# A bank of its own for the third product of a group's first pair, and a norm whose stream waits for GpSimd by a price

## The chip, the cores and the metric

The kernel runs on one core of one Trainium2 chip. The time is device microseconds of one launch. A core has a matrix engine (TensorE, PE in the profile; PEld is its loading of weights), VectorE (DVE), ScalarE (ACT), GpSimd (POOL), SyncE (SP, which here only starts transfers) and 16 DMA engines. Each engine works through its own list of instructions in the order in which the program was written; engines wait for each other by semaphores.

## What is computed

One layer of a streaming encoder for 512 prompt rows and 8 x 16 sample rows, 640 rows together, with 1024 channels in 32-bit floats:

```python
z = x @ w_in                                  # x is layer-normed; columns: xa, ya, glu, q, gates
out_a = (rg_lru(causal_conv(xa, width 4)) * gelu(ya)) @ proj_a
u = glu[:512] * sigmoid(glu[512:])            # D_CONV = 512 channels
v = causal_conv(u, width 31)
out_b = silu(layer_norm(v)) @ proj_b          # norm over the 512 channels
out_c = cross_attention(q, memory) @ proj_c   # 4 heads, 256 tokens; the samples have caches of their own
g = sigmoid(gates + b_gate)
x = layer_norm(alpha * x + (g0 * out_a + g1 * out_b + g2 * out_c) @ w_out)
x = layer_norm(alpha * x + (silu(x @ w_ffn_gate) * (x @ w_ffn_up)) @ w_ffn_down)
```

## The kernel before

Activations lie with channels on the 128 partitions and the 640 rows along the free axis, in two halves of 320 (`HT`). Each 32-bit operand is split into a high part, rounded to a shorter format, and a low part, the rest; a product is three matmuls (high x high, high x low, low x high). The split inputs are `xh` and `xl`; the split weights `wh` and `wl`, made of a loaded block `wr`: ScalarE copies the high part (`prep_hi`) and VectorE, in some steps GpSimd (L305), subtracts to get the low part (`prep_lo`).

The work of TensorE is a list of `Step` objects. A main loop goes through it: it prepares the weights of the steps to come, issues this step's matmuls, and issues its evacuation (`evac`) a while later. An ordinary step multiplies one block of weights by both halves and takes two PSUM banks, `pu`, of four. There is a second kind of tile, `pv`, with two banks each, of which there are two; `side` counts those in use, `room` waits for one and `over` gives one back.

The small work (convolutions, norms, softmax, recurrence) is written as streams, which are Python generators. After each piece of matmuls the loop calls `advance`. It holds a price for every instruction that is written and so a time for TensorE (`P`), VectorE (`V`) and ScalarE (`A`); it takes a stream on as long as the larger of the times of V and A lies behind P's. At a `yield None` a stream stops until the next call. The prices only decide the order in which instructions are written; on the chip semaphores decide when they run. GpSimd (`G`) has no price before the change.

Two places matter.

First, `ln_b_stream`, the norm over the convolution's channels, around 253 us of the span. `total` adds up four tiles of 128 x 640 on GpSimd (L853 and L855). The stream stops once, and then writes a product of the sum with `ones` on TensorE, which spreads the mean over the partitions. VectorE subtracts that from the tiles, ScalarE squares them, GpSimd adds up the squares, and after two stops a second product follows (five matmuls of 128 x 100), then a power on GpSimd and `token_row`, a set of transposes.

Second, `seven`. The gates and the FFN's products are done in pairs of two blocks of columns by a scheme with seven products instead of eight (Strassen's, in Winograd's form): m1 to m7, each of 12 matmuls of 128 x 320, eight with the high part of a weight and four with its low part. Some products are accumulated in one bank. `after` says what happens to each product: m1 is copied by ScalarE into `tmp["a"]`; m6 is added to that copy by VectorE, m7 to the result, and `put` writes the four quarters of the output, with a function (sigmoid for the gates, SiLU for the FFN's gate) by ScalarE at the end. A group's first pair (`first`; the gates' at 491 us, the FFN's at 686 us) has an order of its own: m1, m4, m2, m6, m5, m7, m3. There m2 goes on in the bank of m1 ("x", `opens` False): its first matmul may only run when ScalarE has copied m1, and ScalarE takes the function of the sum from that bank.

```python
    PRODUCTS = (("m1", "x", True, "11", "11"), ("m6", "y", True, "s2", "t2"), ("m2", "x", False, "12", "21"),
...
            products = [PRODUCTS[i] for i in (0, 5, 2, 1, 4, 3)] + [("m3", "x", True, "s4", "22")]
```

Of the kernel before, what the change touches and what calls it, by code (L numbers as in the profile page):

```python
# [11 lines left out]
OP = mybir.AluOpType  # L12
# [8 lines left out]
HT = T // 2  # L21
# [46 lines left out]
def elements(x):  # L68
    n = 1
    for d in x.shape[1:]:  # L70
        n *= d
    return n
# [10 lines left out]
    return (130 if name == "scalar_tensor_tensor" else 70) + n / 0.96  # L83


TABLES = {AF.Exp: "e", AF.Tanh: "esgl", AF.Sigmoid: "s", AF.Sqrt: "q", AF.Silu: "l", AF.Gelu_apprx_tanh: "g"}


# [21 lines left out]
class Slots:  # L110
# [7 lines left out]
    def get(self, shape, dtype=F32):  # L118
        if not self.free_list:
            raise RuntimeError("no slot is free")  # L120
        i = self.free_list.pop(0)
        self.low = min(self.low, len(self.free_list))
        self.count += 1
        x = self.pool.tile([128, T], dtype, name=f"s{i}_{self.count}", tag=f"s{i}", bufs=1)
        x = view(x, shape)
        self.at[id(x)] = (i, x)
        return x
# [16 lines left out]
def trunk(ctx, tc, x_prompt, x_sample, mem_prompt, state_conv_a, state_lru, state_conv_b, cache_mem_k, cache_mem_v,  # L144
# [4 lines left out]
          new_conv_a_s, new_lru_s, new_conv_b_s):  # L149
    nc = tc.nc  # L150
    V, A, P = Engine(nc.vector, price_vector), Engine(nc.scalar, price_scalar), Engine(nc.tensor, price_tensor)
    G, S = nc.gpsimd, nc.sync

    w_in, proj_a, proj_b, proj_c, w_out = w_in[0], proj_a[0], proj_b[0], proj_c[0], w_out[0]
    w_mem_k, w_mem_v = w_mem_k[0], w_mem_v[0]
# [21 lines left out]
    side = [0]  # L177

    def pv():
        assert side[0] < 2  # L180
        side[0] += 1
        return ps.tile([128, 2, 512], F32, name="pv", tag="v", bufs=2)

    def room(n=1):
        while side[0] + n > 2:
            yield None

    def over(n=1):
        side[0] -= n
# [126 lines left out]
    def flush():  # L316
        while pending:
            pending.pop(0)()
# [5 lines left out]

    def advance(few=False):

        for e in (V, A):
            e.time = max(e.time, state["since"])
        state["since"] = P.time
        for item in list(streams):  # L330
            name, gen = item
            if few and name not in often:
                continue
            while max(V.time, 0 if name in vector_next else A.time) < P.time:
                try:
                    c = next(gen)
                except StopIteration:
                    streams.remove(item)
                    done.add(name)
                    break  # L340
                vector_next.discard(name)
                if c is None:
                    break
                if c == "v":
                    vector_next.add(name)

    def until(cond):

        flush()
        for item in list(streams):  # L350
            while not cond():
                try:
                    next(item[1])
                except StopIteration:
                    streams.remove(item)
                    done.add(item[0])
                    break
        assert cond()
# [391 lines left out]
    first = {"glu": len(steps)}  # L750
# [99 lines left out]
    def ln_b_stream():  # L850
        def total(x):
            y = get([128, T])
            G.tensor_tensor(y, x[0], x[1], op=OP.add)  # L853
            for k in range(2, KC):
                G.tensor_tensor(y, y, x[k], op=OP.add)  # L855
            return y

        y = total(vb)
        yield 1
        yield None  # L860
        yield from room()
        p = pv()
        P.matmul(p[:, 0], ones, y[:, :512], start=True, stop=True)
        P.matmul(p[:, 1, :128], ones, y[:, 512:], start=True, stop=True)
        free(y)
        yield None
        over()
        sq = []
        for k in range(KC):
            V.tensor_sub(vb[k][:, :512], vb[k][:, :512], p[:, 0])  # L870
            V.tensor_sub(vb[k][:, 512:], vb[k][:, 512:], p[:, 1, :128])
            x = get([128, T])
            A.activation(x, vb[k], AF.Square)
            sq.append(x)
            yield 1
        y = total(sq)
        free(*sq)
        yield 1
        yield None
        yield None  # L880
        yield from room()
        p = pv()

        for t in range(5):
            P.matmul(p[:, 0, t * 100:(t + 1) * 100], y[:, t * 128:(t + 1) * 128], ones[:, :100], start=True, stop=True)
        free(y)
        yield None
        over()
        ve = small.tile([128, 5], F32, name="ve5")
        V.tensor_scalar(ve, p[:, 0, :500].rearrange("p (t n) -> p t n", n=100)[:, :, 0], EPS, None, op0=OP.add)  # L890
        rs = small.tile([128, 5], F32, name="rs5")
        G.tensor_tensor(rs, ve, mhalf[:, :5], op=OP.pow)
        yield 1
        yield from room()
        p = token_row(rs)
        yield None
        over()
        for k in range(KC):
            V.tensor_mul(vb[k][:, :512], vb[k][:, :512], p[:, 0])
            V.tensor_mul(vb[k][:, 512:], vb[k][:, 512:], p[:, 1, :128])  # L900
            yield 1
        for k in range(KC):
            A.activation(vb[k], vb[k], AF.Silu, scale=pb[:, k, 32:33], bias=pb[:, k, 33:34])
        yield 1
        for k in range(KC):
            hi, lo = get([128, T], F32R), get([128, T], F32R)
            split(hi, lo, vb[k])
            free(vb[k])
            bT[k] = (hi, lo)
            yield 1  # L910
# [596 lines left out]
    def seven(pair, put, following, first=False):  # L1507

        acc, tmp, late = {}, {}, []

        def fourth(p):
            put(0, 1, p, tmp["b"][:, 0], OP.subtract)

        def fifth(p):
            put(1, 1, p, tmp["b"][:, 0], OP.add)
            if first:
                V.tensor_tensor(tmp["a"][:, 1], tmp["a"][:, 1], p, op=OP.add)

        def after(n, p):
            if n == "m1":  # L1520
                tmp["a"], tmp["b"] = get([128, 2, HT]), get([128, 2, HT])
                copy(tmp["a"][:, 0], p)
            elif n == "m6":
                V.tensor_tensor(tmp["a"][:, 1], tmp["a"][:, 0], p, op=OP.add)
            elif n == "m2":
                put(0, 0, p, None, None)
            elif n == "m7":
                V.tensor_tensor(tmp["b"][:, 0], tmp["a"][:, 0], p, op=OP.add)
                for f in late:
                    f()  # L1530
            elif n in ("m4", "m5"):
                f = lambda: (fourth if n == "m4" else fifth)(p)
                if first:
                    late.append(f)
                else:
                    f()
            else:
                free(tmp["b"])
                put(1, 0, p, tmp["a"][:, 1], OP.add)
                free(tmp["a"])  # L1540

        products = PRODUCTS
        if first:

            products = [PRODUCTS[i] for i in (0, 5, 2, 1, 4, 3)] + [("m3", "x", True, "s4", "22")]
        for i, (n, u, opens, xn, wn) in enumerate(products):
            def mm(w, u=u, opens=opens, xn=xn):
                if opens:
                    acc[u] = pu(1)[0][:, :HT]
                p = acc[u]  # L1550
                hi, lo = w
                xhi, xlo = quarters[xn]
                for k in range(half):
                    P.matmul(p, hi[:, k], xhi[k], start=opens and k == 0, stop=False, skip_group_check=not opens)
                    P.matmul(p, hi[:, k], xlo[k], start=False, stop=False, skip_group_check=not opens)
                yield
                for k in range(half):
                    P.matmul(p, lo[:, k], xhi[k], start=False, stop=k == half - 1, skip_group_check=not opens)
                yield

            before = None
            if first and i == 0:
                before = sums_there
            elif first and i == 2 and following:
                before = lambda: (following.sums_1(), following.sums_2())
            elif following and not first and i == 2:
                before = following.sums_1
            elif following and not first and i == 3:
                before = following.sums_2
            Step(pair.ld, (lambda r, wn=wn: pair.block(wn)), [128, half, 128], mm,  # L1570
                 (lambda n=n, u=u: after(n, acc[u])), before=before, half=parity[0] % 2,
                 after=lambda wn=wn: pair.drop(wn))
            parity[0] += 1
# [253 lines left out]
    for tiles in ((0, 1, 2), (3, 4)):  # L1827
# [4 lines left out]
        acc = {}  # L1832
# [126 lines left out]
```

## Time and profile before

| | before |
|---|---|
| runs, us | 1099.13, 1100.48, 1100.15 |
| median, us | 1100.15 |
| profiled execution, us | 1099.67 |
| its span, first to last instruction, us | 1097.9 |
| granted clock of TensorE, mean | 0.99 |
| TensorE busy | 97% of the span |
| VectorE, ScalarE, GpSimd busy | 73%, 45%, 15% |

All times of places are microseconds from the span's start. In a row of the timeline stand the start, the length of the group, the engine, the line, the operation with its output and input tiles, shapes and count, and in brackets the idle time of that engine just before and what ended it. Nearly all instructions have line 64, which is the place where `Engine` issues them; so tiles and shapes say which is which: `pu` and `pv` are PSUM tiles, `s` a work tile. A list of waits has, for each engine, what it waited for: us in total, times, longest. A table of stretches has the stretch, its length, and busy time and number of instructions of PE, PEld, DVE, ACT and POOL, then the granted clock (1.00 is full speed), the DMA engines' share and GB/s. A row of the chain of waits has start, length, engine, tile and count.

### The profile page before, as it was taken

How to read it: one execution, taken by the hardware profiler on the slowest of the kernel's cores; microseconds unless marked ns; L12 is line 12 of the kernel's file. 1: busy time of each engine (PE TensorE's matmuls, PEld its weight loads, DVE VectorE, ACT ScalarE, POOL GpSimd, SP SyncE). 2: the span in 40 equal slices, each digit the busy share in tenths (PEclk: the TensorE clock that was granted, in tenths of full speed). 3: DMA queues.
4: the chain of work that ended last, by engine and by line, in shares of the span. 5: the costliest groups of instructions: out<-in, count | busy, mean ns of one | idle time of the engine just before them, and what ended most of it. 6: DMA issues, size and time to landing. Idle time of an engine off the chain costs nothing.

```text
span 1097.9 us, 17000 instructions
## 1 busy us (share of the span) xinstructions
PE 1061.7 (97%) x6827; PEld 1005.9 (92%) x6827; DVE 802.9 (73%) x1335; ACT 490.1 (45%) x863; POOL 165.3 (15%) x185
## 2 busy tenths in 40 slices
PE   8799898998999999999999999899999999999997
PEld 6699898997999999999999889899999999888886
DVE  6929898996364873779855678888887887544775
ACT  4532645446648445846523124433444444334341
POOL 3623323556200000010001120000000000100111
PEclk9999999998999999999999999999999999999999
DMA  9732123352412121212325331132222322734481
GB/s 340 253 95 78 39 67 97 118 154 65 147 52 83 59 96 59 95 45 78 115 78 172 135 134 59 39 101 92 77 78 85 108 77 78 287 115 137 162 289 45
DMA packets 80334, 123.11 MB, mean 112 GB/s; under 512 B 4075, under 2 KB 59371, under 8 KB 80256
## 3 DMA queue, kind: packets, MB, share of 16 engines
q1 hardware_dynamic: 73168, 100.36, 27.6%
q0 software_dynamic: 7088, 21.68, 6.2%
q8 instruction: 53, 0.87, 0.3%
q14 instruction: 25, 0.20, 0.1%
HBM read 112.41 MB, written 9.61 MB: 111 GB/s over the span
## 4 chain that ended last, share of the span: by engine, by line
PE 70%; DVE 11%; ACT 4%; issue 1%; DVEq 0%; ACTq 0%
PE pu L64 62%; DVE s L64 10%; PE pv L64 8%; ACT s L64 3%; ACT L64 1%; DVE wl L64 1%; ACT wh L64 0%; DVE xres L64 0%; DVE mx L64 0%; DVE wh L64 0%; DVE xl L64 0%; DVE nm L64 0%; DVEq L1955 0%; ACT wl L64 0%; DVE st L64 0%
## 5 line engine op out<-in xcount | busy, mean ns | idle before, releaser
L64 PE MATMUL pu<-xh,wh 128*128 128x320 f32 x1040 | 252.6, 315 | 8.3 <-ACT s L64 7.1
L64 PE MATMUL pu<-xh,wl 128*128 128x320 f32 x1040 | 246.9, 310 | 0.0
L64 ACT ACTIVATE wh<-wr 128x1024 fp32r<-128x1024 f32 (+1 forms) x149 | 134.9, 908 | 229.1 <-PE pu L64 123.2
L64 PE MATMUL pu<-xl,wh 128*128 128x320 f32 x888 | 219.7, 311 | 0.0
L64 PEld LDWEIGHTS pu<-xh,wh 128*128 128x128 f32 x1040 | 178.1, 190 | 13.2 <-ACT s L64 9.1
L64 PE MATMUL pu<-s,wh 128*128 128x320 f32 x1064 | 185.5, 310 | 1.9 <-DVE s L64 1.3
L64 PEld LDWEIGHTS pu<-xh,wl 128*128 128x128 f32 x1040 | 177.4, 189 | 0.1
L64 DVE TENSOR_TENSOR s<-s,s 128x640 fp32r<-128x640 f32 (+4 forms) x176 | 124.5, 723 | 65.5 <-ACT s L64 63.3
L64 PEld LDWEIGHTS pu<-s,wh 128*128 128x128 f32 x1064 | 163.4, 188 | 3.4 <-DVE s L64 2.4
L64 DVE TENSOR_TENSOR wl<-wr,wh 128x1024 fp32r<-128x1024 f32 (+1 forms) x100 | 114.1, 1141 | 66.7 <-ACT wh L64 66.7
L64 PEld LDWEIGHTS pu<-xl,wh 128*128 128x128 f32 x888 | 154.2, 189 | 0.6 <-DVE xl L64 0.6
L64 DVE TENSOR_TENSOR s<-s,pu 128x320 f32<-128x320 f32 x188 | 88.4, 484 | 85.8 <-PE pu L64 83.3
L64 PE MATMUL pu<-s,wl 128*128 128x320 f32 x808 | 147.3, 310 | 0.9 <-DVE s L64 0.9
L64 DVE SCALAR_TENSOR_TENSOR s<-s,pb,s 128x511 f32<-128x511 f32 (+14 forms) x240 | 130.1, 613 | 7.8 <-ACT s L64 7.8
L64 ACT ACTIVATE s<-s 128x640 fp32r<-128x640 f32 (+4 forms) x144 | 87.9, 629 | 101.9 <-DVE s L64 101.8
L64 PEld LDWEIGHTS pu<-s,wl 128*128 128x128 f32 x808 | 126.1, 188 | 1.1 <-issue 1.1
L64 PE MATMUL pu<-wh,s 128*128 128x512 f32 (+1 forms) x396 | 116.2, 386 | 0.3 <-ACT wh L64 0.3
L64 PEld LDWEIGHTS pu<-wh,s 128*128 128x128 f32 x396 | 73.1, 189 | 15.1 <-ACT wh L64 1.2
L64 ACT ACTIVATE s<-pu 128x320 f32<-128x320 f32 (+2 forms) x90 | 36.7, 442 | 68.1 <-PE pu L64 68.0
L64 PE MATMUL pu<-wl,s 128*128 128x512 f32 (+1 forms) x198 | 62.9, 389 | 1.6 <-POOL wl L305 0.8
L305 POOL TENSOR_TENSOR wl<-wr,wh 128x1024 fp32r<-128x1024 f32 x13 | 44.4, 3418 | 81.2 <-ACT wh L64 68.4
L64 PE MATMUL pv<-wh,s 128*128 128x512 f32 (+1 forms) x152 | 48.7, 367 | 0.4 <-DVE xres L64 0.4
(139 smaller groups left out, 1249.0 us busy)
## 6 DMA issues: line engine op xcount, KB each, us to landing
wr<-in_w_in SPq DMA_DIRECT2D x26, 1024.0 KB, 5.1
wr<-in_w_ffn_down SPq DMA_DIRECT2D x19, 1024.0 KB, 5.1
wr<-in_w_ffn_gate SPq DMA_DIRECT2D x11, 1024.0 KB, 5.3
wr<-in_w_ffn_up SPq DMA_DIRECT2D x11, 1024.0 KB, 5.3
s<-in_cache_mem_k POOLq DMA_DIRECT2D x16, 256.0 KB, 7.0
s<-in_cache_mem_v POOLq DMA_DIRECT2D x16, 256.0 KB, 7.2
wr<-in_proj_a SPq DMA_DIRECT2D x4, 1024.0 KB
wr<-in_w_out SPq DMA_DIRECT2D x4, 1024.0 KB, 5.7
```

The source lines that it names most:

```text
L64: return f(*a, **k)
L305: self.eng.tensor_tensor(l, x, f32(h), op=OP.subtract)
```

## The change

GpSimd becomes an engine with a price: 600 for the start of a transfer, else 150 and 3.2 for each element of a partition. `settle(engine)` stops a stream until the priced time of TensorE has reached that engine's. In the norm it stands in place of the fixed stops after the two sums, and once more after the power. In `seven`, m2 of a group's first pair opens a `pv` tile; `put` adds it to `tmp["a"][:, 0]`, the copy of m1, on VectorE, and ScalarE takes the function of that sum out of SBUF.

```diff
--- before.py
+++ after.py
@@ -83,6 +83,12 @@
     return (130 if name == "scalar_tensor_tensor" else 70) + n / 0.96
 
 
+def price_pool(e, name, a, k):
+    if name == "dma_start":
+        return 600
+    return 150 + 3.2 * elements(a[0])
+
+
 TABLES = {AF.Exp: "e", AF.Tanh: "esgl", AF.Sigmoid: "s", AF.Sqrt: "q", AF.Silu: "l", AF.Gelu_apprx_tanh: "g"}
 
 
@@ -149,7 +155,7 @@
           new_conv_a_s, new_lru_s, new_conv_b_s):
     nc = tc.nc
     V, A, P = Engine(nc.vector, price_vector), Engine(nc.scalar, price_scalar), Engine(nc.tensor, price_tensor)
-    G, S = nc.gpsimd, nc.sync
+    G, S = Engine(nc.gpsimd, price_pool), nc.sync
 
     w_in, proj_a, proj_b, proj_c, w_out = w_in[0], proj_a[0], proj_b[0], proj_c[0], w_out[0]
     w_mem_k, w_mem_v = w_mem_k[0], w_mem_v[0]
@@ -324,7 +330,7 @@
 
     def advance(few=False):
 
-        for e in (V, A):
+        for e in (V, A, G):
             e.time = max(e.time, state["since"])
         state["since"] = P.time
         for item in list(streams):
@@ -343,6 +349,13 @@
                     break
                 if c == "v":
                     vector_next.add(name)
+
+    def settle(*engines):
+
+        t = max(e.time for e in engines or (V, A))
+        yield None
+        while P.time < t:
+            yield None
 
     def until(cond):
 
@@ -850,6 +863,7 @@
     def ln_b_stream():
         def total(x):
             y = get([128, T])
+            G.time = max(G.time, V.time, A.time)
             G.tensor_tensor(y, x[0], x[1], op=OP.add)
             for k in range(2, KC):
                 G.tensor_tensor(y, y, x[k], op=OP.add)
@@ -857,7 +871,7 @@
 
         y = total(vb)
         yield 1
-        yield None
+        yield from settle(G)
         yield from room()
         p = pv()
         P.matmul(p[:, 0], ones, y[:, :512], start=True, stop=True)
@@ -876,8 +890,7 @@
         y = total(sq)
         free(*sq)
         yield 1
-        yield None
-        yield None
+        yield from settle(G)
         yield from room()
         p = pv()
 
@@ -891,6 +904,7 @@
         rs = small.tile([128, 5], F32, name="rs5")
         G.tensor_tensor(rs, ve, mhalf[:, :5], op=OP.pow)
         yield 1
+        yield from settle(G)
         yield from room()
         p = token_row(rs)
         yield None
@@ -1523,7 +1537,11 @@
             elif n == "m6":
                 V.tensor_tensor(tmp["a"][:, 1], tmp["a"][:, 0], p, op=OP.add)
             elif n == "m2":
-                put(0, 0, p, None, None)
+                if first:
+                    put(0, 0, p, tmp["a"][:, 0], OP.add)
+                    over()
+                else:
+                    put(0, 0, p, None, None)
             elif n == "m7":
                 V.tensor_tensor(tmp["b"][:, 0], tmp["a"][:, 0], p, op=OP.add)
                 for f in late:
@@ -1543,9 +1561,13 @@
         if first:
 
             products = [PRODUCTS[i] for i in (0, 5, 2, 1, 4, 3)] + [("m3", "x", True, "s4", "22")]
+            products[2] = ("m2", "v", True, "12", "21")
         for i, (n, u, opens, xn, wn) in enumerate(products):
             def mm(w, u=u, opens=opens, xn=xn):
-                if opens:
+                if u == "v":
+                    until(lambda: side[0] < 2)
+                    acc[u] = pv()[:, 0, :HT]
+                elif opens:
                     acc[u] = pu(1)[0][:, :HT]
                 p = acc[u]
                 hi, lo = w
```

TensorE and GpSimd have as many instructions as before; VectorE gets two more, and ScalarE has two table loads fewer. SyncE's order is unchanged. Between 250 and 490 us many rows of VectorE and ScalarE change places.

TensorE at the norm's first product. `wh_2499` and `wl_2500` are the weights of one step, `wh_2610` and `wl_2611` those of the next; `s15_162_2714` is GpSimd's sum. Before:

```order
L64 MATMUL pu_2721<-xh_83,wl_2500 128x320
L64 MATMUL pu_2722<-xh_83,wl_2500 128x320
L64 MATMUL pv_2766<-s15_162_2714,ones_81 128x512 [waits PE_49,Pool_49]
L64 MATMUL pv_2766<-s15_162_2714,ones_81 128x128
L64 MATMUL pu_2721<-xh_83,wh_2499 128x320
...
L64 MATMUL pu_2722<-xh_83,wl_2500 128x320
L64 MATMUL pu_2814<-xh_83,wh_2610 128x320 [waits Activation_49]
L64 MATMUL pu_2815<-xh_83,wh_2610 128x320 [waits Activation_49]
```

After:

```order
L64 MATMUL pu_2722<-xh_83,wl_2500 128x320
L64 MATMUL pu_2721<-xh_83,wh_2499 128x320
...
L64 MATMUL pu_2722<-xh_83,wl_2500 128x320
L64 MATMUL pu_2803<-xh_83,wh_2610 128x320 [waits Activation_49]
L64 MATMUL pu_2804<-xh_83,wh_2610 128x320 [waits Activation_49]
...
L64 MATMUL pu_2804<-xh_83,wl_2611 128x320
L64 MATMUL pv_2841<-s15_162_2714,ones_81 128x512 [waits PE_49,Pool_49]
L64 MATMUL pv_2841<-s15_162_2714,ones_81 128x128
L64 MATMUL pu_2803<-xh_83,wh_2610 128x320
```

The product with `ones` moved behind 48 matmuls: the second half of one step and the first half of the next, whose two banks wait for ScalarE.

ScalarE at the same place, which reads alike in both programs but for the numbers. The exponentials of a softmax (`nm` is the negative maximum from VectorE) stand ahead of the sigmoid that empties `pu_2613` and `pu_2614`. After:

```order
L64 ACTIVATE wh_2718<-wr_2432 128x1024 [waits DMAHW2_49,PE_49,Pool_49]
L64 ACT_TABLE_LOAD [waits DMASW1_49,DVE_49]
L64 ACTIVATE s48_163_2752,sm_2751<-pv_2223,nm_2749 128x256 [waits PE_49]
L64 ACTIVATE s48_163_2752,sm_2751<-pv_2223,nm_2749 128x256
L64 ACTIVATE s30_164_2753,sm_2751<-pv_2223,nm_2749 128x256 [waits DMASW2_49]
L64 ACTIVATE s30_164_2753,sm_2751<-pv_2223,nm_2749 128x256
L64 ACT_TABLE_LOAD
L64 ACTIVATE s31_169_2766<-pu_2613,pa_85 128x320 [waits DMASW3_49]
L64 ACTIVATE s31_169_2766<-pu_2614,pa_85 128x320
```

Nothing moved here; the rows tell what the banks wait for.

ScalarE in the first pair of the gates. `pu_5205` holds m1 before, `pu_5230` after: the table load and the row with `pa_85` behind it are for the function of the sum that m2 completes. Before:

```order
L64 ACTIVATE wl_5219<-s2_284_5021 128x512
L64 ACTIVATE s9_306_5230<-pu_5205 128x320 [waits PE_49]
L64 ACTIVATE wh_5238<-s49_285_5023 128x512 [waits Activation_49]
L64 ACTIVATE wl_5261<-s34_283_5019 128x512
L64 ACT_TABLE_LOAD [waits PE_49]
L64 ACTIVATE s43_312_5272<-pu_5205,pa_85 128x320 [waits Activation_49]
L64 ACTIVATE wh_5279<-wr_4836 128x512
L64 ACTIVATE wl_5299<-wr_4983 128x512 [waits DMAHW3_49]
```

After:

```order
L64 ACTIVATE wl_5244<-s33_294_5068 128x512
L64 ACTIVATE s47_316_5256<-pu_5230 128x320 [waits PE_49]
L64 ACTIVATE wh_5264<-s4_295_5070 128x512
L64 ACTIVATE wl_5288<-s40_293_5066 128x512
L64 ACT_TABLE_LOAD [waits DVE_49]
L64 ACTIVATE s41_322_5299<-s41_322_5299,pa_85 128x320 [waits Activation_49]
L64 ACTIVATE wh_5307<-wr_4877 128x512
L64 ACTIVATE wl_5326<-wr_5034 128x512 [waits DMAHW3_49,PE_49]
```

The table load for the sigmoid waited for TensorE and now waits for VectorE; the cast of the last product's weights (`wh` from `wr`) stands behind the function in both.

VectorE there, around the evacuations of m2 and m6. Before:

```order
L64 TENSOR_TENSOR wl_5261<-s34_283_5019,wl_5261 128x512 [waits PE_49,Activation_49]
L64 TENSOR_TENSOR s15_271_4730<-s13_208_3293,s29_270_4729 128x640
L64 TENSOR_TENSOR s9_306_5230<-s9_306_5230,pu_5263 128x320 [waits PE_49]
L64 TENSOR_TENSOR wh_5279<-wr_4836,wh_5279 128x512 [waits Activation_49]
L64 TENSOR_TENSOR s10_220_3443<-s10_220_3443,s21_273_4766 128x640
L64 TENSOR_TENSOR wl_5299<-wr_4983,wl_5299 128x512 [waits Activation_49]
```

After:

```order
L64 TENSOR_TENSOR wh_5264<-s4_295_5070,wh_5264 128x512 [waits PE_49,Activation_49]
L64 TENSOR_TENSOR s41_322_5299<-s47_316_5256,pv_5274 128x320 [waits PE_49]
L64 TENSOR_TENSOR wl_5288<-s40_293_5066,wl_5288 128x512 [waits Activation_49]
L64 TENSOR_TENSOR s47_316_5256<-s47_316_5256,pu_5290 128x320 [waits PE_49]
L64 TENSOR_TENSOR wh_5307<-wr_4877,wh_5307 128x512 [waits Activation_49]
L64 TENSOR_TENSOR s15_259_4342<-s15_259_4342,s21_310_5183 128x640
L64 TENSOR_TENSOR wl_5326<-wr_5034,wl_5326 128x512 [waits Activation_49]
```

An add of the `pv` tile to the copy of m1 (`s47_316_5256`) came in ahead of a product's low weights (`wl_5288`) and the evacuation of m6.

## The prediction

> **What bounds the kernel.** I read the page first, then the list of waits of TensorE, then the timeline around the three places that the change touches.
>
> ```profile
> span 1097.9 us, 17000 instructions
> ...
> PE 1061.7 (97%) x6827; PEld 1005.9 (92%) x6827; DVE 802.9 (73%) x1335; ACT 490.1 (45%) x863; POOL 165.3 (15%) x185
> ...
> PE 70%; DVE 11%; ACT 4%; issue 1%; DVEq 0%; ACTq 0%
> ```
>
> ```profile
> PE pu L64 <- ACT s L64: 7.6, 4, 4.3
> PE pv L64 <- POOL s L855: 5.0, 1, 5.0
> ```
>
> TensorE works for 97% of the span, and its instructions are the same in number before and after. So the change can only move idle time of TensorE and the stretches at half clock that follow an idle time. The two longest waits are one of 5.0 us for GpSimd's sum of the norm and one of 4.3 us for ScalarE; the change is aimed at both. Everything that the other engines gain or lose counts only where TensorE waits for it.
>
> **A. The norm's first product.** The columns of the next rows are start, length, engine, line, operation and, in brackets, the idle time ahead and what ended it; in the table of stretches they are the length, then the busy time of PE, PEld, DVE, ACT and POOL, the granted clock and the DMA.
>
> ```profile
> 253.17 2.50 PE L64 MATMUL pv<-s,ones 128*128 128x512 f32 x4 [5.00 <-POOL s L855]
> ...
> 253.21 1.28 ACT L64 ACT_TABLE_LOAD   x1 [8.90 <-DVE nm L64]
> 256.45 1.28 ACT L64 ACT_TABLE_LOAD   x1
> 257.75 0.95 ACT L64 ACTIVATE s<-pu,pa 128x320 f32<-128x320 f32 x2
> ...
> 326.46 3.52 PE pu L64 x24
> ...
> 248.17:263.38 15.21, 10.21 (x54) 9.17 (x54) 8.16 (x17) 10.13 (x21) 9.44 (x12) 0.78 0.36 105
> 253.17:258.00 4.83, 4.83 (x16) 3.79 (x17) 2.63 (x6) 4.75 (x11) 4.83 (x8) 0.56 0.68 193
> ```
>
> Before, TensorE stops at 248.17, starts the product at 253.17 and then runs at half clock: 4.83 x (1 - 0.56) = 2.1 us are lost. The 15.21 us to 263.38 hold 5.00 of waiting, 2.1 of slow clock, two groups of 24 matmuls (3.52 each by the chain's row) and 1.07 of the product (what is left). After, the two groups stand ahead of the product. The first group needs nothing new and ends at 248.17 + 3.52 = 251.69. The second opens the banks that ScalarE's sigmoid at 257.75 empties: there are four banks, two for a step, and its banks are those of two steps earlier. On ScalarE nothing changes up to that row: the softmax stands ahead of the sigmoid, and it waits for VectorE's maximum (the 8.90 us at 253.21), with a table load on each side. So the second group starts at 257.75 + 0.95 = 258.7, and TensorE waits 7.0 us in place of 5.0. The slow clock comes back too, and its price is the term of which least is known.
>
> ```profile
> 136.82 0.74 PE L64 MATMUL pu<-xh,wh 128*128 128x320 f32 x2 [2.30 <-ACT s L64]
> ...
> 136.82:142.20 5.38, 5.38 (x25) 5.23 (x26) 5.38 (x10) 2.93 (x6) 3.34 (x1) 0.68 0.00 0
> 694.12:697.36 3.24, 3.24 (x12) 3.24 (x13) 3.21 (x6) 0.99 (x2) 0.00 (x0) 0.53 0.00 0
> ```
>
> The losses after waits of 2.30 and 4.32 us are 5.38 x 0.32 = 1.7 and 3.24 x 0.47 = 1.5. I take 1.6; the ends are 0.75 (half of the shortest, if the wait ends inside a slow stretch that is about to end) and 2.1. The two groups, the wait, the product and the loss come to 3.52 + 7.0 + 3.52 + 1.07 + 1.6 = 16.7 against 15.21: **+1.5, from +0.7 to +2.1**.
>
> **B. What stands behind the norm's product.** The small products of the sample rows' values need ScalarE's copies of the probabilities. After the change these copies stand on ScalarE behind three squares of the norm, which stand behind VectorE's subtractions, and these behind six taps of a convolution.
>
> ```profile
> 258.58 1.70 ACT L64 ACTIVATE s<-s,rc 128x256 f32<-128x256 f32 x4
> 261.44 1.05 ACT L64 ACTIVATE wh<-wr 128x1024 fp32r<-128x1024 f32 x1
> 262.39 1.14 ACT L64 ACTIVATE s<-s 128x512 fp32r<-128x512 f32 x2
> 266.62 0.91 ACT L64 ACTIVATE s<-s,pa 128x640 f32<-128x640 f32 x1
> 269.06 1.19 ACT L64 ACTIVATE s<-pv 128x256 f32<-128x256 f32 x4
> ...
> 264.27 1.67 DVE L64 TENSOR_TENSOR s<-s,pv 128x512 f32<-128x512 f32 x4
> 267.56 6.32 DVE L64 SCALAR_TENSOR_TENSOR s<-s,pa,s 128x511 f32<-128x511 f32 x6 [1.62 <-ACT s L64]
> 275.67 2.85 DVE L64 SCALAR_TENSOR_TENSOR s<-s,pa,s 128x511 f32<-128x511 f32 x6
> ...
> 269.69 2.45 POOL L305 TENSOR_TENSOR wl<-wr,wh 128x1024 fp32r<-128x1024 f32 x1
> ...
> 271.98 1.08 PE L64 MATMUL pv<-s,s 128*32 128x128 f32 x32
> ```
>
> The same number of matmuls stands ahead of these products, so TensorE comes to them at 271.98 + 1.5 = 273.5. ScalarE's probabilities end at 260.2; a weight's copy (1.05), the copies of LRU weights (1.14) and the tap's start (0.91) end at 263.3; six taps at 2.85 end at 266.1, four subtractions at 267.8; the last square (0.7), a weight's copy (1.05) and a product with a scale (0.8) lead to 270.4. That is 3.1 us of slack. With the taps at 6.32, as beside GpSimd, 273.9, and TensorE waits 0.4. I take **+0.3**; the ends are 0 and +1.9 (the slow rival below).
>
> **C. The wait at 357.** It comes of a table load on ScalarE ahead of a sigmoid.
>
> ```profile
> 357.26 0.89 PE L64 MATMUL pu<-s,wh 128*128 128x320 f32 x4 [0.87 <-DVE s L64]
> ...
> 355.57 1.28 ACT L64 ACT_TABLE_LOAD   x1
> ```
>
> The order after the norm differs between 260 and 490 us, and there are two table loads fewer in the program. At this place the load no longer stands ahead of the sigmoid: **-0.9, from -0.9 to 0**.
>
> **D. First pair of the gates.** Before, the third product continues in the first one's bank and must wait until ScalarE has copied it; after, it opens a bank of its own, and VectorE adds it to the copy.
>
> ```profile
> 495.30 0.41 PE L64 MATMUL pu<-xh,wh 128*128 128x320 f32 x1 [0.51 <-ACT s L64]
> 501.69 1.99 PE L64 MATMUL pu<-s,wl 128*128 128x320 f32 x12 [0.86 <-DVE s L64]
> 505.28 0.31 PE L64 MATMUL pu<-xh,wl 128*128 128x320 f32 x1
> ...
> 497.41 1.28 ACT L64 ACT_TABLE_LOAD   x1 [1.11 <-PE pu L64]
> 498.70 0.53 ACT L64 ACTIVATE s<-pu,pa 128x320 f32<-128x320 f32 x1
> 499.13 0.62 ACT L64 ACTIVATE wh<-wr 128x512 fp32r<-128x512 f32 x1
> ...
> 499.13 0.68 DVE L64 TENSOR_TENSOR wh<-s,wh 128x512 fp32r<-128x512 f32 x1
> 501.47 0.68 DVE L64 TENSOR_TENSOR wh<-wr,wh 128x512 fp32r<-128x512 f32 x1
> ```
>
> The wait of 0.51 goes. But the sigmoid and its table load, which waited for TensorE only, now wait for VectorE's add, and the cast of the last product's weights stands behind them on ScalarE. VectorE does the add behind the low part at 499.13. That part may come up to 0.51 earlier; I take half, so the add runs from 499.13 - 0.26 + 0.6 = 499.5 to 500.0. Table load, sigmoid and cast (1.28 + 0.53 + 0.62, pipelined by 0.1 twice) end at 502.4, and VectorE's low part for the last product starts there, not at 501.47: 0.95 later, and all that frees the bank which the next pair needs at 505.28 is later with it. **+0.95**. The low end is -1.37, if both waits of these rows go and nothing takes their place; the high end +1.9, if the next step is held up as much again.
>
> **E. First pair of the FFN.**
>
> ```profile
> 694.12 0.51 PE L64 MATMUL pu<-xh,wh 128*128 128x320 f32 x1 [4.32 <-ACT s L64]
> 701.04 1.92 PE L64 MATMUL pu<-s,wl 128*128 128x320 f32 x12
> ...
> 694.00 0.68 DVE L64 TENSOR_TENSOR wh<-wr,wh 128x512 fp32r<-128x512 f32 x1
> 699.48 0.49 DVE L64 TENSOR_TENSOR s<-s,pu 128x320 f32<-128x320 f32 x1 [0.45 <-PE pu L64]
> ```
>
> The wait of 4.32 us mostly stays. The product's eight matmuls with the high parts of its weights no longer wait, but the other four need the low part, which VectorE makes at 694.00 to 694.68 behind work without a gap. So TensorE waits there instead, some 3.9 us. It then has eight matmuls less to do. Later the sixth of the seven products needs VectorE's evacuation at 699.48; that loses its own wait of 0.45 and gets one more add (0.4) ahead of it, so it ends at 699.9 or so, and the product of 701.04 can start 1.15 earlier at most. At half clock TensorE arrives later, and 0.5 is left. I take **-0.8, from -1.15 to -0.5**. [...]
>
> VectorE's two additional adds (0.49 each) and ScalarE's two table loads less (1.28 each) lie beside TensorE's work elsewhere.
>
> **The sum** is 1.5 + 0.3 - 0.9 + 0.95 - 0.8 = +1.05 on the profiled execution's 1099.67. The runs' median, 1100.15, is 0.48 above that execution, so I predict 1101.2. A measurement of this kernel can tell about 0.2% (2.2 us) from no change. The ends of the terms, taken as independent, make 1099.2 to 1103.6.
>
> **The rivals.**
> - Slow: VectorE and GpSimd collide ahead of the values. After, GpSimd makes a weight's low part (2.45 at 269.69) before its memsets and so beside the two LRU subtractions and the six taps. If the taps cost 3.47 more (6.32 for 2.85) and the subtractions twice their 1.3, the copies come at 270.4 + 3.5 + 1.4 = 275.3 against 273.5: 1.8 of waiting, and 1.6 of slow clock on top if it counts like the 2.30 at 136.82. In place of B's 0.3 that is 1102.7 to 1104.3. It decides as soon as that block takes over 3.1 us more than alone. [...]
> - Partly fast: the bank of its own pays as it stands, D at -1.37 and E at -1.15, with A at +0.7, B at 0 and C at -0.9: -2.7, or 1097.4. Against it stands the table load behind the add.
> - Fast: the wait of 5.0 us goes and no other comes. Then A is -5.0 - 2.1 = -7.1 in place of +1.5, and the time 1092.6. It needs the bank empty by 251.69, and the sigmoid's row at 257.75 speaks against it, unless ScalarE's softmax came six us earlier, for which I see no cause.
> - The change does nothing: the old wait of 5.0 is exchanged for one as long. That is A at 0 and lies inside the forecast.
>
> **Chances.** Forecast 0.5, slow 0.3, partly fast 0.12, fast 0.08. Of the forecast's half some 0.05 lies above +0.2%. So faster 0.2, same 0.45, slower 0.35. The range reaches from the partly fast case, 1097.4, to the slow one's end, 1104.3.
>
> **What the profile after would show.** A: no wait for GpSimd's line at 253, but one of about 7 us of an x matmul for ScalarE, from 251.7 to 258.7. B: the 32 small products without a wait, or with one for ScalarE. C: no wait near 357. D: the add from a pv bank near 499.5, and the next pair's first matmul a microsecond late. E: a wait of some 3.9 us at a matmul with wl, not with wh. I am wrong if TensorE doesn't idle between 251.7 and 258, or if the places between 290 and 490, whose order changed as well, hold new waits of microseconds.

## The result, and the profile after

The changed kernel takes 1105.51 us (median of five runs, 1104.41 to 1106.11) against 1099.75 for the kernel before (median of five, the three runs of the earlier table and two more). The ratio is 1.005, with a 95% interval from 1.0036 to 1.0063: slower by half a per cent. The forecast was 1101.2, with no change that can be measured as the likeliest outcome.

The page after, in its span, busy time and chain of waits:

```profile
span 1103.7 us, 17003 instructions
...
PE 1061.6 (96%) x6827; PEld 1006.5 (91%) x6827; DVE 808.9 (73%) x1337; ACT 486.5 (44%) x861; POOL 166.1 (15%) x185
...
PE 68%; DVE 13%; ACT 4%; issue 2%; DVEq 0%; ACTq 0%
```

TensorE is as busy as before to a tenth of a microsecond (1061.7 then), and the span is 5.8 us longer. So all of the loss is time in which TensorE does nothing. The list of TensorE's waits after, in us in total, times and longest:

```profile
PE pu L64 <- ACT s L64: 11.2, 5, 6.6
PE pv L64 <- DVE wh L64: 5.8, 2, 3.8
...
PE pu L64 <- DVE s L64: 2.8, 3, 1.2
```

The wait for GpSimd's sum (5.0) is gone, and ScalarE's are up from 7.6 to 11.2; the waits for `wh`, weights that VectorE has not finished, are new. Where they lie is seen in TensorE's timeline after, of which only rows with a wait are shown:

```profile
259.06 1.05 PE L64 MATMUL pu<-xh,wh 128*128 128x320 f32 x2 [6.63 <-ACT s L64]
...
429.21 1.12 PE L64 MATMUL pu<-s,wh 128*128 128x320 f32 x4 [0.76 <-ACT s L64]
491.04 0.42 PE L64 MATMUL pu<-xh,wh 128*128 128x320 f32 x1 [0.58 <-ACT s L64]
496.03 0.41 PE L64 MATMUL pv<-xh,wh 128*128 128x320 f32 x1 [1.20 <-ACT wh L64]
499.50 0.86 PE L64 MATMUL pv<-xh,wh 128*128 128x320 f32 x4 [2.03 <-DVE wh L64]
503.97 0.85 PE L64 MATMUL pu<-xh,wh 128*128 128x320 f32 x4 [0.69 <-DVE wh L64]
505.46 2.00 PE L64 MATMUL pu<-s,wl 128*128 128x320 f32 x12 [0.64 <-DVE s L64]
510.41 0.38 PE L64 MATMUL pu<-xh,wl 128*128 128x320 f32 x1 [1.19 <-DVE s L64]
515.06 0.41 PE L64 MATMUL pu<-xh,wl 128*128 128x320 f32 x1 [0.90 <-ACT s L64]
700.67 1.43 PE L64 MATMUL pv<-xh,wh 128*128 128x320 f32 x4 [3.77 <-DVE wh L64]
```

One wait stands at the norm and one in the FFN's first pair, both about as forecast. Six stand between 496 and 515 us, in the gates' first two pairs, where there were two short ones (0.51 and 0.86). The table sets the stages side by side. Its marks are starts of rows in TensorE's timeline of each profiled execution: the product at 187.57 before, the first of the values' small products (271.98), the first matmul of the gates' first pair (491.10) and of its second (505.28), and the same two for the FFN (686.12, 704.56). A stage is the difference of two marks, in us.

| kernel | to 188 | norm, to the values | to the gates | gates' first pair | between | FFN's first pair | rest |
|---|---|---|---|---|---|---|---|
| before | 187.57 | 84.41 | 219.12 | 14.18 | 180.84 | 18.44 | 393.34 |
| after | 188.32 | 85.10 | 217.62 | 19.37 | 181.64 | 18.72 | 392.93 |
| bank_only | 188.04 | 84.39 | 219.12 | 14.57 | 180.70 | 19.14 | 392.94 |
| settle_only | 188.30 | 86.01 | 217.57 | 18.35 | 180.41 | 19.69 | 392.87 |
| hold | 187.77 | 86.35 | 216.84 | 16.09 | 181.11 | 17.89 | 393.25 |
| hold_need | 187.88 | 86.24 | 216.80 | 12.32 | 180.51 | 19.65 | 394.00 |

The gates' first pair costs 5.2 us more after the change (19.37 against 14.18), and the pair behind it another 0.8 ("between"). The norm's 0.7 are more than given back on the way to the gates (-1.5). The first column differs by 0.75 between the two, ahead of everything that the change touches; it lies between 187.20 and 188.47 in the thirteen kernels of this document, and differs as much between kernels that are alike up to there. From left to right the differences are +0.75, +0.69, -1.50, +5.19, +0.80, +0.28 and -0.41, together the 5.8 us of the span.

What the pair waits for is read from ScalarE and VectorE. ScalarE after, around the pair's start:

```profile
489.93 0.74 ACT L64 ACTIVATE s<-s 128x640 fp32r<-128x640 f32 x1 [1.69 <-DVE s L64]
490.57 0.75 ACT L64 ACTIVATE s<-pu 128x320 f32<-128x320 f32 x2
492.29 0.74 ACT L64 ACTIVATE s<-s 128x640 fp32r<-128x640 f32 x1 [0.97 <-DVE s L64]
494.72 0.74 ACT L64 ACTIVATE s<-s 128x640 fp32r<-128x640 f32 x1 [1.69 <-DVE s L64]
495.36 0.61 ACT L64 ACTIVATE wh<-wr 128x512 fp32r<-128x512 f32 x1
495.88 0.74 ACT L64 ACTIVATE s<-pu 128x320 f32<-128x320 f32 x2
496.52 1.36 ACT L64 ACTIVATE xh<-s 128x640 fp32r<-128x640 f32 x2
```

VectorE after, at the same place:

```profile
490.70 1.56 DVE L64 TENSOR_TENSOR s<-s,s 128x640 fp32r<-128x640 f32 x2 [0.26 <-ACT s L64]
493.06 1.56 DVE L64 TENSOR_TENSOR s<-s,s 128x640 fp32r<-128x640 f32 x2 [0.81 <-ACT s L64]
497.29 1.56 DVE L64 TENSOR_TENSOR xl<-s,xh 128x640 fp32r<-128x640 f32 x2 [2.66 <-ACT xh L64]
498.76 0.68 DVE L64 TENSOR_TENSOR wh<-wr,wh 128x512 fp32r<-128x512 f32 x1
```

The two engines hand a piece to and fro. VectorE multiplies the recurrence's output with its gate, ScalarE casts it, VectorE takes the low part, and only then does the next multiplication stand in VectorE's list: 2.4 us for each piece (489.93, 492.29, 494.72), with both engines idle for part of it. Six such casts, from 482.73 to 494.72, stand on ScalarE ahead of the sum and the weights that the pair needs, and on VectorE the six multiplications with five of the low parts. So m2's high weights are cast at 495.36 and TensorE waits 1.20 for them. The rows with `xh` and `xl` are the high and low parts of the last of the sums of the input's quarters, written over a quarter of the input; they are forced ahead of the pair's weights. The high part starts at 496.52, where before it started at 493.06; the low part and m2's low weights follow at 497.29 and 498.76, and TensorE waits another 2.03. Before, seven of the eight casts of the recurrence's pieces stood inside the pairs, from 502.98 to 537.43, between rows that were wanted first. ScalarE before, the sum's high part and two of these casts:

```profile
493.06 1.35 ACT L64 ACTIVATE xh<-s 128x640 fp32r<-128x640 f32 x2
...
502.98 0.74 ACT L64 ACTIVATE s<-s 128x640 fp32r<-128x640 f32 x1 [2.71 <-DVE s L64]
...
514.10 0.74 ACT L64 ACTIVATE s<-s 128x640 fp32r<-128x640 f32 x1 [2.21 <-DVE s L64]
```

They can stand earlier now since the recurrence ends earlier: its last scan on VectorE,

```profile
478.85 1.49 DVE L64 TENSOR_TENSOR_SCAN s<-s,s 128x640 f32<-128x640 f32 x1
```

before, is at 453.11 after:

```profile
453.11 1.49 DVE L64 TENSOR_TENSOR_SCAN s<-s,s 128x640 f32<-128x640 f32 x1
```

The stream of these products (`a_stream`) takes whatever is ready, and knows nothing of what the pair needs.

### The profile page after: what moved, and what is told of

Read it like the earlier page. It is cut to its first block, busy times and chain, and to the rows that moved or that the text cites. A ratio compares the mean times of both kernels' runs of the same rounds, so it can differ in the third digit from the quotient of the medians.

```text
span 1103.7 us, 17003 instructions
## 1 busy us (share of the span) xinstructions
PE 1061.6 (96%) x6827; PEld 1006.5 (91%) x6827; DVE 808.9 (73%) x1337; ACT 486.5 (44%) x861; POOL 166.1 (15%) x185
## 4 chain that ended last, share of the span: by engine, by line
PE 68%; DVE 13%; ACT 4%; issue 2%; DVEq 0%; ACTq 0%
PE pu L64 60%; DVE s L64 11%; PE pv L64 8%; ACT s L64 2%; ACT L64 1%; ACT wh L64 1%; DVE wl L64 1%; DVE xres L64 0%; DVE mx L64 0%; DVE wh L64 0%; DVE nm L64 0%; DVE xl L64 0%; DVEq L1977 0%; ACT xh L64 0%; DVE st L64 0%
## 5 line engine op out<-in xcount | busy, mean ns | idle before, releaser
L64 PE MATMUL pu<-xh,wh 128*128 128x320 f32 x1024 | 247.0, 313 | 11.2 <-ACT s L64 9.5
L64 PE MATMUL pu<-xl,wh 128*128 128x320 f32 x880 | 217.0, 310 | 0.0
L64 PEld LDWEIGHTS pu<-xh,wh 128*128 128x128 f32 x1024 | 174.3, 189 | 15.5 <-ACT s L64 10.3
```

What stands on the lines that cost most here:

```text
L64: return f(*a, **k)
```

## The experiments

All medians are of runs beside the kernel before on the same chip (1100.06 to 1100.18 there); ratios are to that kernel, with their 95% interval.

| kernel | what it is | median, us | ratio |
|---|---|---|---|
| bank_only | only m2's own bank | 1100.41 | 1.0002 (0.9993 to 1.0011) |
| settle_only | only GpSimd's price and `settle` | 1103.65 | 1.0034 (1.0021 to 1.0046) |
| hold | the change, recurrence's products held | 1100.82 | 1.0005 (0.9996 to 1.0013) |
| hold_early | hold, one evacuation earlier | 1102.39 | 1.0019 (1.0011 to 1.0028) |
| hold_now | hold, three evacuations earlier | 1103.03 | 1.0027 (1.0017 to 1.0037) |
| bank_late | bank_only, all sums ahead of m6 | 1102.16 | 1.0019 (1.0010 to 1.0028) |
| hold_now_late | hold_now, and all sums ahead of m6 | 1100.37 | 1.0002 (0.9994 to 1.0011) |
| bank_need | bank_only, sums piece by piece | 1102.81 | 1.0022 (1.0013 to 1.0031) |
| hold_need | hold, sums piece by piece | 1099.04 | 0.9986 (0.9977 to 0.9995) |
| before_need | before, sums piece by piece | 1101.52 | 1.0014 (1.0005 to 1.0023) |
| hold_gates | hold, sums piece by piece in the gates alone | 1095.83 | 0.9961 (0.9947 to 0.9974) |

**Which half it is.** bank_only takes the diff's parts in `seven`, settle_only all the others.

> Only the half of the change in seven: m2 of a first pair in a bank of its own, added to the copy of m1; GpSimd has no price and the norm its fixed stops. Theory 1 (the loss of some 5 us in the gates' first pair comes of five products of the gated recurrence, multiply, cast and low part, which the prices moved ahead of that pair; the bank itself costs little): 1099 to 1101, with the gates' first pair starting its next pair's first matmul at 505 to 506.3. Theory 2 (the bank of its own makes the loss, since the add and the table load stand ahead of the last product's weights): 1104 to 1106.

> Only the other half: GpSimd has a price and the norm's stream waits by it; m2 goes on in m1's bank as before. Theory 1: about 1105, the whole loss, with the products of the recurrence ahead of the first pair. Theory 2: 1099 to 1101.

The bank alone changes nothing that can be measured, and its gates' first pair takes 14.57 us, 0.4 more than before. The price alone makes 3.5 us of loss at the median, and its pair takes 18.35, where TensorE's longest wait there is one for ScalarE's copy of m1, behind the same pieces:

```profile
499.61 0.42 PE L64 MATMUL pu<-xh,wh 128*128 128x320 f32 x1 [3.94 <-ACT s L64]
```

So theory 1 holds for the half that it names. The median is some 1.4 below "about 1105", and below its own profiled execution (1105.01); with the bank as well the pair takes one more microsecond.

**Whether it is the recurrence's products.**

```diff
             while j not in hs or j not in gel:
                 yield None
+            while state["i"] < first["pairs"] + 0:
+                yield None
             h = hs.pop(j)
```

> The whole change, but the stream that multiplies the recurrence's output with its gate and splits it may not write its products before the gates' pairs begin, so that these stand behind the first pair's weights and inputs; nothing is left out. Theory 1: 5 to 6 us less than the changed kernel, 1099.5 to 1100.5. Theory 2: no change, 1105.

4.7 us less than the changed kernel, all else kept. The gates' first pair falls from 19.37 to 16.09, the stage behind it from 181.64 to 181.11, and the sum's high part starts on ScalarE at 491.67, ahead of the recurrence's casts:

```profile
491.02 0.77 ACT L64 ACTIVATE s<-pu 128x320 f32<-128x320 f32 x2 [5.76 <-PE pu L64]
491.67 1.37 ACT L64 ACTIVATE xh<-s 128x640 fp32r<-128x640 f32 x2
494.77 0.74 ACT L64 ACTIVATE s<-s 128x640 fp32r<-128x640 f32 x1 [1.73 <-DVE s L64]
```

This shows the cause of most of the loss: 3.3 of the pair's 5.2 us and 0.5 of the 0.8 behind it. The rest of what the median falls by lies in stages where the slow clock varies (in the profiled execution the FFN's first pair is 0.8 shorter and the norm 1.3 longer) and is not explained. At 1100.82 the median lies a little above the forecast of 1099.5 to 1100.5. The pair is still 1.9 above before, with held pieces standing within it now (the casts at 494.77 and 497.14 on ScalarE).

**What the wait at the norm is for.** hold_early writes the sigmoid that frees the banks ahead of the softmax; hold_now writes three steps' evacuations as soon as the step ends.

```diff
# hold_early, in the main loop
+            if i == 30:
+                flush()
             advance()
# hold_now, in the main loop
-            if s.now:
+            if s.now or i in (29, 30, 31):
                 flush()
```

> As the one before, and one evacuation, the sigmoid that frees the banks for the step behind the norm's product, is written on ScalarE ahead of the softmax rather than behind it. If the wait of 6.6 us at 259 is for that row, it shrinks to the 1.5 us until GpSimd's sum is there, and the clock may stay up: 4 to 7 us less than the one before, 1093 to 1096. Rival: the values' copies or the probabilities become the next wait and hold nearly all of it: within 1.5 us of the one before.

> The whole change with the recurrence's products held as in hold, and the evacuations of three steps around the norm's product written at once when their step ends, so that neither the softmax nor the norm's squares stand ahead of them on ScalarE. If the banks are what TensorE waits for at 259 (and at 269 with one evacuation moved), only the 1.5 us for GpSimd's sum at 253 remain: 4 to 6 us less than hold, 1095 to 1097. Rival: the copies of the probabilities for the values become the next wait: within 1.5 us of hold.

Both gains failed to come. In hold_early the wait for ScalarE does shrink to 1.48 for GpSimd, as the forecast of the wait's cause says, and 16 us later another step's banks wait as long:

```profile
253.28 1.35 PE L64 MATMUL pv<-s,ones 128*128 128x512 f32 x4 [1.48 <-POOL s L64]
269.06 1.05 PE L64 MATMUL pu<-xh,wh 128*128 128x320 f32 x2 [6.52 <-ACT s L64]
```

In hold_now no bank waits, but the values' small products do:

```profile
254.03 1.35 PE L64 MATMUL pv<-s,ones 128*128 128x512 f32 x4 [1.44 <-POOL s L64]
271.13 1.93 PE L64 MATMUL pv<-s,s 128*32 128x128 f32 x32 [7.83 <-ACT s L64]
```

That wait is for ScalarE's copies of the probabilities, at 270.72 behind the norm's squares. The product with `ones` starts at 265.03 in hold and at 253.28 and 254.03 in these two, some 11 to 12 us earlier. The copies only move from 272.44 to 269.32 and 270.72; before, they come at 269.06. So near the norm the chain over VectorE, ScalarE and GpSimd sets most of the time, and an earlier TensorE mostly waits later. The waits are 5.0 us before, 6.65 in hold, 1.48 + 6.52 = 8.0 in hold_early and 1.44 + 7.83 = 9.3 in hold_now.

The two kernels are 1.6 and 2.2 slower than hold, a little more than the rivals' 1.5. The rival of hold_now named the next wait; in hold_early it was another bank's and not the copies'. The longer waits are not all of the difference: from the first mark to the gates' pair these two take 0.7 and 1.5 us more than hold. In both, the FFN's first pair takes 1.2 more (19.06 and 19.05 against 17.89), with the same wait of 3.77 but a longer slow stretch (some 6 us against 3.4, by the pace of the matmuls).

**The sums of the input's quarters.** In each first pair the sums that are still missing are forced ahead of the first product (`sums_there`). bank_late forces them ahead of m6, and bank_need each ahead of the product that reads it:

```diff
# bank_late
-            if first and i == 0:
+            if first and i == 3:
                 before = sums_there
# bank_need, hold_need, before_need
-            if first and i == 0:
+            if first and i in (3, 4, 5):
+                before = lambda xn=xn: sums_until(xn)
+            elif first and i == 6:
                 before = sums_there
```

`sums_until` takes the stream of the sums on until the quarter `xn` is there.

> Only m2's own bank, as in bank_only, and in both first pairs the sums of input quarters that are still missing are forced ahead of the fourth product (m6, the first that reads one) rather than ahead of the first; nothing is left out. If m2's wait of 3.8 us in the FFN is for its weights' low part, which stands on VectorE behind those sums, that wait and its slow stretch go: 2.5 to 5 us less than bank_only, 1095.5 to 1098. Rival: VectorE is the limit there (15.9 of 18.4 us busy before) and a later product waits as long: within 1 us of bank_only.

> hold_now and the later sums of bank_late together: both places are apart, so the two gains add up, 1090 to 1094, below both kernels. Rival: VectorE's work in the first pairs takes one of them back: 1095 to 1098.

> Only m2's own bank, and each sum of input quarters forced no earlier than ahead of the product that reads it (s2 ahead of m6, s1 ahead of m5, s3 ahead of m7, s4 ahead of m3), where the kernels force all of them ahead of a first pair's first product; nothing is left out. The wait of 3.8 us for m2's low part came back as 4.5 us for the evacuation of m6 when all sums were forced ahead of m6. If it is their standing in one piece that delays whatever is behind it on VectorE, then spread out they delay nothing: the FFN's first pair takes 13 to 14 us in place of 18 to 19, and the time is 1094 to 1097. Rival: VectorE has too much work in the pair whatever the order, and the wait comes a third time, at m3: within 1.5 us of bank_only's 1100.4.

> The kernel before, with m2 in m1's bank, and the sums forced piece by piece as in bank_need. If m2 waited for ScalarE's copy of m1 only because that copy stood behind casts of those sums, the bank of its own is worth nothing here: 1094 to 1097, within 1 us of bank_need. Rival: the shared bank still costs a wait for the copy in each first pair: 1 us or more above bank_need.

> The whole change, the recurrence's products held until the gates' pairs, and the sums forced piece by piece as in bank_need. If both causes are what they are taken for, the loss of the change is gone and the FFN's wait too: 1094 to 1097, as bank_need. If GpSimd's price costs anything else, it stays above bank_need by that, 1 us or more.

None of these five came out as forecast. bank_late and bank_need are 1.8 and 2.4 above bank_only, more than their rivals allow; hold_now_late lies above both of its ranges; before_need is 1.3 below bank_need, as neither of its cases has it; hold_need is 2 above its range. In the FFN the wait moved each time and did not shrink. It stands at m2's low weights in bank_only, at the product m7, for m6's evacuation, in bank_late, and at m3 in bank_need:

```profile
695.45 1.43 PE L64 MATMUL pv<-xh,wh 128*128 128x320 f32 x4 [3.77 <-DVE wh L64]
```

```profile
700.23 3.31 PE L64 MATMUL pu<-s,wl 128*128 128x320 f32 x12 [4.53 <-DVE s L64]
```

```profile
702.42 0.49 PE L64 MATMUL pu<-s,wh 128*128 128x320 f32 x1 [3.40 <-ACT s L64]
703.99 3.30 PE L64 MATMUL pu<-s,wh 128*128 128x320 f32 x11 [1.07 <-DVE s L64]
```

That pair takes 18.7 to 19.7 us in these kernels. The bank is not what decides there: before_need waits the same 3.40 at m3 without it. In the gates it went otherwise, in the kernels that also have the hold: 12.32 us in hold_need, against 14.52 in bank_need and 13.80 in before_need. No kernel has the hold without GpSimd's price, or the price and the late sums without the hold, so it stays open which of these two the late sums need beside them. The two gains expected of hold_now_late could not add up, since neither place gave its own. Its total is still 2.7 below hold_now, and the gates' first pair is 12.32 us there too, against 16.07 in hold_now. hold_need is the first kernel below before, by 1.1 us.

**Both put together.** hold_gates takes hold and the sums piece by piece for the gates' pairs only.

> As hold_need, but the sums are forced piece by piece in the gates' first pair alone; in the FFN's they stand ahead of its first product as in the kernels. The gates' first pair took 12.3 us in hold_need and 16.1 in hold, the FFN's 19.7 and 17.9. If the two places are independent, the time is that of hold less 3.8: 1096 to 1098, below both kernels. Rival: what the FFN's pair takes is mostly the phase of the slow clock, and nothing is gained over hold_need: 1098.5 to 1099.5.

1095.83 us, at the low edge of the forecast of 1096 to 1098: 4.3 below before, and 9.7 below the changed kernel's median. The gates' first pair runs without a gap:

```profile
490.25:502.57 12.32, 12.32 (x86) 12.32 (x85) 9.17 (x16) 7.65 (x14) 0.00 (x0) 1.00 0.16 51
```

TensorE is busy for all of 12.32 us, at full clock, where before it was busy for 12.81 of 14.18. The FFN's pair keeps its 3.77 us wait and takes 18.75. The step from hold is 5.0, more than the 3.8 of the gates; where the other 1.2 comes from is open.

## Why the prediction was wrong

**The step that failed is D**, the gates' first pair: +0.95 with ends at -1.37 and +1.9, measured +5.2, and +0.8 in the pair behind it. Its sum went through the rows inside the pair, each with the time at which it stood before, and moved the add's surroundings earlier by half of 0.51. What stood ahead of the pair on ScalarE and VectorE was taken as unchanged. But the order there had changed, as the text on the change says in one sentence, and in D that sentence had no price. A reader of the order alone could have priced it: six pieces of a multiplication, a cast and a low part in a row, with little between, at some 0.8, 0.74 and 0.8 us by rows of the profile before. hold shows what this step left out: with these pieces behind the pair's first rows, 3.3 of the 5.2 us go. The closing remark, that new waits between 290 and 490 would make the prediction wrong, named the region whose order had changed; the new waits stand just behind it, from 496 on.

D's own sum has a slip that changes little: an add that ends at 500.0 and then 1.28 + 0.53 + 0.62, less 0.1 twice, make 502.2 and not 502.4, so +0.75. Taken alone, D's mechanism was there and its size near: in bank_only, where nothing ahead of the pair moves, the pair costs 0.4 more (14.57 against 14.18), and the wait of 0.51 goes while the one at m7 grows from 0.86 to 1.37:

```profile
502.53 2.00 PE L64 MATMUL pu<-s,wl 128*128 128x320 f32 x12 [1.37 <-DVE s L64]
```

**A held.** A wait of 6.63 for ScalarE's sigmoid, ending at 259.06, in place of 5.00 for GpSimd: forecast 7.0, ending at 258.7. The stage became 0.7 to 1.9 us longer in the four kernels of the table with the price, against +1.5 with ends at 0.7 and 2.1. Its term for the slow clock was in part luck. A slow stretch is counted here, as in the forecast, at its length times what the granted clock lacks to 1.00. That is a little too much: before, the FFN's matmuls of 128 x 320 follow each other every 0.27 us at a clock of 0.50 (694.43 to 696.30) and every 0.15 at full clock, which makes 0.45 of the length and not 0.50. From the wait's end to 268 us the count is 8.94 x 0.17 = 1.5 after the change, for a forecast of 1.6. In settle_only and hold, with waits of 6.64 and 6.65, the matmuls keep the slow pace for 5.5 and 6.3 us, and half of that is 2.8 and 3.1, above the term's upper end of 2.1.

**B held**: the small products don't wait after the change (273.42, without a bracket). Their slack was smaller than forecast, though: the copies start at 273.00, not at 270.4. The slow rival put the loss here, at GpSimd beside VectorE; with 1102.7 to 1104.3 it came nearest to the 1105.5 measured, but its loss did not occur here. The two subtractions did take 3.08 in place of 1.31 (263.04 before), beside GpSimd's low part (2.40 at 262.04), and the six taps took 2.85, as those at 275.67 before:

```profile
262.51 3.08 DVE L64 TENSOR_TENSOR s<-s,s 128x512 fp32r<-128x512 f32 x2 [5.13 <-ACT s L64]
265.52 2.85 DVE L64 SCALAR_TENSOR_TENSOR s<-s,pa,s 128x511 f32<-128x511 f32 x6
```

**C held in its place**: the wait of 0.87 at 357 is gone, and the one of 0.46 at 379 with it, though the one at 429 grew from 0.43 to 0.76. From the values to the gates the kernel gains 1.5 us; 0.5 of it is less waiting (1.9 before, 1.3 after), and where the rest comes from is open.

**E had the mechanism, and its gain is smaller than what the slow clock varies by.** The wait moved from m2's high weights to its low ones, 3.77 us for a forecast of 3.9. After these two waits the granted clock is 0.50; before, for 3.41 us, and after, for 5.29:

```profile
694.30:697.71 3.41, 3.41 (x14) 3.41 (x15) 3.38 (x6) 0.92 (x3) 0.00 (x0) 0.50 0.00 0
```

```profile
700.67:705.96 5.29, 5.29 (x20) 5.29 (x21) 5.25 (x10) 1.55 (x4) 0.00 (x0) 0.50 0.00 0
```

That is 1.7 us lost against 2.6. Less these losses, the pair takes 16.7 us before and 16.1 after, a gain of some 0.6 for a forecast of 0.8; with them it is 0.3 slower. The other kernels with these two waits agree: less its loss, the pair takes 16.6 with the shared bank (settle_only) and 16.0 to 16.2 with the bank of its own (bank_only, hold, hold_early, hold_now, hold_gates), while the loss itself goes from 1.7 to 3.1 us. settle_only, with the same wait of 4.32 as before, takes 19.69 against 18.44. What sets the length of the slow stretch after one and the same wait is not shown by these runs.

## What to carry to other kernels

When a change shifts the order in which small work is written, price the rows ahead of the place that waits, not only the rows in it; pieces that two engines hand to and fro one after the other cost their whole round trip (2.4 us a piece here). Work that is not wanted soon should be held until something else stands between its pieces, and work that is wanted soon, such as sums, can be written just ahead of its reader; in the gates, with the hold, that removed every wait of the first pair (12.32 us for 16.09), in the FFN it moved the wait to the next reader (3.40 us at m3). Where a stage is bound by another engine's chain, removing one of TensorE's waits there can move it to the next reader (at the norm 6.65 us of waiting became 8.0 and 9.3): look for what the wait's end stands on before sending the work earlier.

## What was not expected of the hardware

The same wait can cost over a microsecond more in one kernel than in another by the clock alone. In the FFN's first pair settle_only and before both wait 4.32 us, and the slow stretch behind it costs 3.1 us in the one and 1.7 in the other (pairs of 19.69 and 18.44). Six kernels wait 3.77 us there, and their pairs take 17.89 to 19.14. A difference of that size at such a place can't be read from one profiled execution. The runs of one kernel spread as well: the eleven of hold_need fall into two groups, four from 1096.56 to 1097.40 with a mean granted clock of 0.991 to 0.994, and seven from 1098.95 to 1099.84, all but one at 0.988. So hold_need's median and its profile (1099.17) are of the slower group, and the fastest of its runs come close to the slowest of hold_gates (1096.53).
